# Loading the first block of a row sum in two DMAs, of 16 and of 112 partitions

One core of one Trainium2 chip runs the kernel. The metric is device time in microseconds (us), median over runs; lower is better.

## The reference

```python
x = np.random.randn(32, 512, 1024).astype(np.float32)   # 67.1 MB
multiplier = 0.5
def reference(x, multiplier):
    return (np.sum(x, axis=-1) * multiplier).astype(np.float32)
```

16,384 rows of 1024 numbers are summed. Every byte is read once and next to nothing is written (the page of before: 67.11 MB read, 0.07 MB written), so the time is about the time to read 67.1 MB.

## The kernel before

Each of the 128 partitions owns 112 consecutive rows, read in seven blocks of 16 rows (64 KB a partition, 8.4 MB a block), and 16 more rows that are read in smaller pieces at the end. (A partition is one of the 128 parts of SBUF, the memory on the chip; HBM is the memory that the input lies in. DMA engines copy from one to the other.) Three buffers rotate. VectorE reduces a block in one instruction; ScalarE helps at the end. The first three loads are moved ahead of the start-up code so that they are issued at once.

```python
    x_pool = ctx.enter_context(tc.tile_pool(name="x", bufs=3))
    ...
    for b in range(n_blocks - 1):
        c0 = b * B                                    # B = 16
        t = x_pool.tile([P, B, D], fp32, name="xb")
        loads.append(nc.sync.dma_start(out=t, in_=x_rows[:, c0 : c0 + B, :]))
        h = B if b < n_blocks - 2 else B // 2
        nc.vector.reduce_sum(
            out=sums[:, c0 : c0 + h], in_=t[:, 0:h, :], axis=mybir.AxisListType.X
        )
        nc.vector.tensor_single_scalar(...)           # times the multiplier
        ...                                           # ScalarE takes rows of the last full block
    ...                                               # the last 16 rows a partition: pieces of 8, 5, 2 rows,
                                                      # then the last row in two parts; two stores
    nc.at_finalize(start_loads_at_entry)              # loads that wait for nothing go first
```

## Time and profile before

| | before |
|---|---|
| time, median of 6 runs | 162.07 us (161.98 to 162.21) |
| span of the profiled run | 160.2 us |
| share of the 16 DMA engines that is busy | 97.6% |
| VectorE busy | 119.3 us (74%) |
| start of the first reduction | 21.83 us |
| packets of 64 KB (one partition of one block) after the first of each engine | 2.418 us (median; the longest 2.55) |

The last row is from the trace's record of DMA packets: a packet here is one partition's 64 KB of a block. The records give each packet's start and duration, not its engine or partition. The lines of the page, the timeline and the stretches are shown and read in the prediction. Two more lines are wanted for comparison: of the page the rate in 40 equal slices of the span, and of the timeline the last reduction:

```profile
GB/s 262 524 524 262 524 524 262 524 524 262 524 524 262 524 491 295 524 458 327 524 409 376 524 344 442 524 262 524 524 262 524 524 262 524 393 393 425 409 410 81
137.93 8.69 DVE L100 TENSOR_REDUCE sums<-xb 128x8 f32<-128x8192 f32 x1 [1.92 <-DMA xb<-in_x_dram]
```

A slice is 4 us and packets count in the slice where they start, so 16 packets come as 262, 32 as 524. The pattern 262, 524, 524 is a steady rate of some 437 on average, near the 16 x 27.1 = 434 of the prediction, and the rate keeps about that level from the first slice to the last but one.

### The profile page before, as it was taken

What the parts mean: (1) busy time and instruction counts of PE and PEld (TensorE: products, weight loads), DVE (VectorE), ACT (ScalarE), POOL (GpSimd) and SP (SyncE); (2) the same over time, 40 slices, a digit from 0 to 9 for tenths busy, and PEclk for the clock granted to TensorE, in tenths of its full rate; (3) what the DMA queues carried; (4) which work ended last, traced back from release to release, by engine and by line L of the source; (5) the groups of instructions that cost most, each with busy time, mean ns of one, the idle gap of its engine ahead of it and who ended that gap; (6) DMA issues with size and microseconds to landing.
All of it is one profiled execution on the core that took longest, in us unless ns stands there. A gap on an engine that the chain in (4) does not pass through costs nothing.

```text
span 160.2 us, 139 instructions
## 1 busy us (share of the span) xinstructions
DVE 119.3 (74%) x35; ACT 17.3 (11%) x31; POOL 0.2 (0%) x4
## 2 busy tenths in 40 slices
DVE  0000059997799968999599995999959999597443
ACT  0000000000000000000000000000000000599952
POOL 0000000000000000000000000000000000000000
DMA  7996996996996996997998979969969969999992
GB/s 262 524 524 262 524 524 262 524 524 262 524 524 262 524 491 295 524 458 327 524 409 376 524 344 442 524 262 524 524 262 524 524 262 524 393 393 425 409 410 81
DMA packets 2016, 67.18 MB, mean 419 GB/s; under 512 B 480, under 2 KB 608, under 8 KB 736
## 3 DMA queue, kind: packets, MB, share of 16 engines
q1 hardware_dynamic: 2016, 67.18, 97.6%
HBM read 67.11 MB, written 0.07 MB: 419 GB/s over the span
## 4 chain that ended last, share of the span: by engine, by line
DMA 75%; DVE 22%; SPq 1%; issue 0%; DVEq 0%
DMA xb<-in_x_dram 51%; DMA end<-in_x_dram 24%; DVE sums L100 22%; SPq L117 1%; DVE end L84 1%; SPq L98 0%; DVE res L103 0%; DVEq L63 0%; DVEq L208 0%
## 5 line engine op out<-in xcount | busy, mean ns | idle before, releaser
L100 DVE TENSOR_REDUCE sums<-xb 128x16 f32<-128x16384 f32 (+1 forms) x7 | 112.0, 16001 | 31.5 <-DMA xb<-in_x_dram 31.5
L74 ACT ACT_TABLE_LOAD x1 | 1.3, 1283 | 138.0 <-DMA xb<-in_x_dram 138.0
L74 ACT ACTIVATE xb<-xb 128x1024 f32<-128x1024 f32 x15 | 15.7, 1044 | 2.1 <-DMA xb<-in_x_dram 2.1
L84 DVE CUSTOM_DVE_ANT_0 xb<-xb 128x512 f32<-128x512 f32 x8 | 5.1, 688 | 5.0 <-DMA xb<-in_x_dram 5.0
L74 ACT ACTIVATION_READ_ACCUMULATOR xb<-xb 128x1 f32 x15 | 2.8, 186 | 0.0
L55 DVE MEMSET end<- 128x2 f32 x1 | 0.1, 60 | 1.8 <-PEq L194 1.8
L103 DVE TENSOR_SCALAR res<-sums 128x16 f32<-128x16 f32 (+1 forms) x7 | 1.2, 174 | 0.2
L84 DVE CUSTOM_DVE_ANT_0 end<-end 128x288 f32<-128x288 f32 (+1 forms) x2 | 0.9, 426 | 0.2
L84 DVE DVE_READ_ACCUMULATOR2_ANT res<- 128x1 f32 x9 | 0.7, 82 | 0.0
L194 POOL MEMSET const-bfloat16-1.0<- 128x1 bf16 x1 | 0.1, 102 | 0.0
L194 POOL MEMSET const-uint8-127<- 128x1 uint8 x1 | 0.1, 101 | 0.0
L194 POOL MEMSET const-float32-0.0<- 128x1 f32 x1 | 0.1, 99 | 0.2 <-issue 0.2
L194 POOL MEMSET const-float32-1.0<- 128x1 f32 x1 | 0.1, 98 | 0.0
L84 DVE DVE_READ_ACCUMULATOR2_ANT end<- 128x1 f32 x1 | 0.1, 82 | 0.0
## 6 DMA issues: line engine op xcount, KB each, us to landing
xb<-in_x_dram SPq DMA_DIRECT2D x1, 4096.0 KB, 31.1
xb<-in_x_dram SPq DMA_DIRECT2D x1, 2560.0 KB, 36.8
xb<-in_x_dram SPq DMA_DIRECT2D x1, 1024.0 KB, 38.9
end<-in_x_dram SPq DMA_DIRECT2D x1, 288.0 KB, 39.1
end<-in_x_dram SPq DMA_DIRECT2D x1, 224.0 KB, 39.1
xb<-in_x_dram SPq DMA_DIRECT2D x7, 40.8
out_dram<-res SPq DMA_DIRECT2D x1, 56.0 KB, 10.0
out_dram<-res SPq DMA_DIRECT2D x1, 8.0 KB, 1.4
```

Source lines behind the costliest of these rows:

```text
L55: nc.vector.memset(end[:, at - 2 : at], 0.0)
L74: acts.append(nc.scalar.activation(out=t[:, r, :], in_=t[:, r, :], func=mybir.ActivationFunctionType.Copy, scale=mul, accum_out=res[:, col ...
L84: return nc.vector.tensor_tensor_reduce(out=row[:, 0:mid], in0=row[:, 0:mid], in1=row[:, mid:], scale=scale, scalar=0.0, op0=ADD, op1=ADD, ...
L100: nc.vector.reduce_sum(out=sums[:, c0 : c0 + h], in_=t[:, 0:h, :], axis=mybir.AxisListType.X)
L103: nc.vector.tensor_single_scalar(out=res[:, c0 : c0 + h], in_=sums[:, c0 : c0 + h], scalar=mul, op=mybir.AluOpType.mult,)
L117: nc.sync.dma_start(out=t[:, lo:hi, :], in_=x_last[:, lo:hi, :])
L194: nc = _bacc.Bacc("TRN2", target_bir_lowering=False, num_devices=1)
```

## The change

The first block is to be loaded by two DMAs: one of 16 partitions, a single row of 64 KB for each DMA engine, and one of the other 112. The idea behind it is that a DMA with few rows is ready sooner, so that the sixteen engines start earlier and more evenly; since the engines are the bound (busy for 97.6% of the span), every idle moment at the start should be paid in full.

```diff
-        loads.append(nc.sync.dma_start(out=t, in_=x_rows[:, c0 : c0 + B, :]))
+        for lo, hi in ((0, 16), (16, P)) if b == 0 else ((0, P),):
+            loads.append(
+                nc.sync.dma_start(
+                    out=t[lo:hi], in_=x_rows[lo:hi, c0 : c0 + B, :]
+                )
+            )
```

## The prediction

> **What bounds the kernel now.** I read the page first: its shares of busy time, the table of DMA queues and the chain that ended last. Columns are explained by the lines themselves; "L" is a source line.
>
> ```profile
> span 160.2 us, 139 instructions
> DVE 119.3 (74%) x35; ACT 17.3 (11%) x31; POOL 0.2 (0%) x4
> q1 hardware_dynamic: 2016, 67.18, 97.6%
> DMA 75%; DVE 22%; SPq 1%; issue 0%; DVEq 0%
> ```
>
> The reader is to see that the DMA engines, at 97.6% of sixteen engines' time, bind, and that VectorE has room. The chain lists VectorE at 22%, but that is only how a chain through a three-buffer ring is followed back: a load is issued when a reduction frees its buffer, and then stands in a queue that is still full. The timeline of VectorE shows the true rhythm (start, duration, then in brackets the idle time before and its releaser):
>
> ```profile
> 21.83 17.22 DVE L100 TENSOR_REDUCE sums<-xb 128x16 f32<-128x16384 f32 x1 [19.96 <-DMA xb<-in_x_dram]
> 41.16 17.22 DVE L100 TENSOR_REDUCE sums<-xb 128x16 f32<-128x16384 f32 x1 [1.90 <-DMA xb<-in_x_dram]
> 60.52 17.22 DVE L100 TENSOR_REDUCE sums<-xb 128x16 f32<-128x16384 f32 x1 [1.94 <-DMA xb<-in_x_dram]
> ```
>
> Every reduction waits about 1.9 us for the DMA. The blocks land 41.16 - 21.83 = 19.33 us apart. A block is 128 partitions of 64 KB, so each of 16 engines moves 8 partition rows: one row takes **T = 19.33 / 8 = 2.416 us**, or 65,536 B / 2.416 us = 27.1 GB/s per engine. The first block lands at 21.83, and 21.83 - 19.33 = 2.5 us is its whole lead-in. I then cut the span into stretches (columns: length, busy time and instructions of DVE, ACT and POOL, clock, DMA share, GB/s; packets count where they start, which is why a stretch can exceed 1):
>
> ```profile
> 0.00:1.00 1.00, 0.00 (x0) 0.00 (x0) 0.20 (x4) 1.00 0.00 0
> 1.00:2.00 1.00, 0.06 (x1) 0.00 (x0) 0.00 (x0) 1.00 3.12 1049
> 21.80:41.20 19.40, 17.44 (x3) 0.00 (x0) 0.00 (x0) 1.00 1.00 432
> 118.50:137.90 19.40, 17.40 (x2) 0.00 (x0) 0.00 (x0) 1.00 0.94 405
> 137.90:157.00 19.10, 14.02 (x19) 16.92 (x30) 0.00 (x0) 1.00 0.98 414
> ```
>
> No data moves in the first microsecond. In the second, 1049 GB/s x 1 us = 1.05 MB start: exactly sixteen rows of 64 KB. All sixteen engines are already at work in that second microsecond, and from then on they never rest: 432 GB/s is 16 x 27.1. The packet records of the trace say it more finely: the sixteen first packets start within 0.51 us of each other, from 1.01 us after the first issue, and take 2.8 to 3.4 us (median 3.13), against 2.42 later. Last, the end of the chain:
>
> ```profile
> 117.89 39.08 DMA end<-in_x_dram
> 156.97 0.02 issue
> 156.99 0.48 DVE end L84 x2
> 157.61 0.39 DVE end L84
> ```
>
> The end hangs directly on the last load; only some 3.2 us follow it up to 160.2. An idle microsecond of the slowest engine anywhere in the run is a microsecond of the total.
>
> [...]
>
> **The change part by part.**
> It removes one DMA of 128 rows and adds one of 16 and one of 112. Bytes and row packets are the same (128 of 64 KB).
>
> Issue: one more DMA on SP, 0.33 us by the issue records, while the engines chew on the first: off the path, 0. VectorE waits for one more semaphore, 0.02 us by the records of such waits. The loads that follow keep their order, and blocks 1 and 2 are still issued at once.[...]
>
> Gain: [...]the stagger of 0.51 us and some of the 3.13 - 2.42 = 0.71 us of slow first packets could go: at most 1.2 us, I'd say 0.3.
>
> Cost, first DMA: [...]**3T = 7.25 us**.
>
> Cost, second DMA: [...]**2T = 4.83 us**. [...] That part rests on exact lockstep, so I take half, **2.4 us**.
>
> After that [...]the lag stays. Block 0 lands about 14 us late, and so does every buffer's release, but three buffers give 2 x 19.33 us of queued work, more than the reduction's 17.22 plus a lag difference of 10, so no engine starves. A reduction still fits in a block's period. Sum: 7.25 + 4.83 + 2.4 - 0.3 = 14.2 us, **162.1 + 14.2 = 176.3 us**.
>
> **The rivals.**
> A, nothing but the lead-in moves. [...]block 0 lands as before: 161.8 to 162.4. [...]
> B, the first DMA alone pays: [...] 162.1 + 7.25 = 169.4, or up to 172 with leftovers.
> C, the 112 are dealt out one by one (row i to engine i mod 16). [...]block 0 takes 8 x 4T = 77 us, 58 us more: 220. [...]
> D, the full lockstep: 3T + 4T = 16.9 us, 179.0.
>
> **The range and the chances.** I give A 0.25, B 0.25, my sum up to D 0.42, C or something else longer 0.08. A holds the result within 2% (3.2 us); B, D and C are all slower by over 2%. Faster by over 2% would need more than the whole 2.5 us of lead-in. Hence 176.3 us, range 161.6 to 181, faster 0.01, same 0.27, slower 0.72.
>
> **What would show it.** Right: the first reduction starts near 36 us, not 21.8; a stretch from 2 to 10 us shows about a quarter of 434 GB/s; the first sixteen packets take some 9.7 us; later gaps between reductions are back near 19.3; VectorE's total wait for the DMA rises by the lag, nearly all of it ahead of the first reduction[...]. If the first packets are long but the reduction starts near 29, B holds; at 77, C. It is wrong if the first reduction still starts near 21.8[...].

The marked passages are cut: which destination partitions slow each other down, and how the rows of a DMA are dealt to the engines; no trace shows it. The sum came to 7.25 + 4.83 + 2.4 - 0.3 = 14.2 us, and 162.1 + 14.2 = 176.3. Its first three terms (3T for the first DMA, 2T for the second, half of another 2T on the way into block 1) stand as what was forecast, not as what any run shows; the 0.3 is a guess.

## The result

| | before | after |
|---|---|---|
| time, median of 6 runs | 162.07 us | 184.08 us (183.53 to 184.36) |
| ratio | | 1.1353 (95% interval 1.1334 to 1.1373) |

A ratio here is the mean time of one kernel's fast runs over that of the other's of the same rounds, so it isn't quite the ratio of the medians. The kernel is 13.5% slower, 22.0 us. Lines of the page of after:

```profile
span 182.3 us, 141 instructions
GB/s 230 14 216 230 244 417 201 230 216 288 446 460 460 460 417 360 403 446 460 446 460 460 431 403 360 446 446 460 446 460 460 417 403 360 439 446 392 431 361 16
q1 hardware_dynamic: 2032, 67.18, 97.1%
```

The same 67.18 MB are moved, and the engines are busy for the same share of a longer span: 97.1%. The busy share therefore says nothing of the loss; the rate does. For the first ten slices (4.56 us each, 46 us) it is about half of what it is later. The timeline of VectorE of after, with the first three reductions and the last, says when the loss occurs:

```profile
44.09 17.22 DVE L106 TENSOR_REDUCE sums<-xb 128x16 f32<-128x16384 f32 x1 [41.55 <-DMA xb<-in_x_dram]
63.35 17.22 DVE L106 TENSOR_REDUCE sums<-xb 128x16 f32<-128x16384 f32 x1 [1.83 <-DMA xb<-in_x_dram]
82.71 17.22 DVE L106 TENSOR_REDUCE sums<-xb 128x16 f32<-128x16384 f32 x1 [1.93 <-DMA xb<-in_x_dram]
...
160.10 8.69 DVE L106 TENSOR_REDUCE sums<-xb 128x8 f32<-128x8192 f32 x1 [1.92 <-DMA xb<-in_x_dram]
```

The first reduction starts 44.09 - 21.83 = 22.3 us later than before. After it the spacing is 19.26 and 19.36 us, as before, and the last one is 160.10 - 137.93 = 22.2 us late. All of the loss falls into the load of the first block; nothing is made up or added later. Stretches of after (the last column is GB/s of packets that start there):

```profile
1.00:2.00 1.00, 0.00 (x0) 0.00 (x0) 0.00 (x0) 1.00 8.57 1049
2.00:8.00 6.00, 0.06 (x1) 0.00 (x0) 0.00 (x0) 1.00 0.00 0
8.00:12.00 4.00, 0.00 (x0) 0.00 (x0) 0.00 (x0) 1.00 1.33 262
```

In the second microsecond sixteen rows start (1.05 MB), as before. Then no engine starts another row for six microseconds; the next sixteen begin between 8 and 12 us. The packet records give the rows of the first block in the order in which each engine took them ("took" is the median of the 16 engines, in us; "last end" is when the slowest engine was done with the row). The records don't name the engine; the rows are strung together by their times, as each starts within 0.03 us of the end of another:

| row of an engine | before: took | after: took | before: last end | after: last end |
|---|---|---|---|---|
| 1 | 3.13 | 8.44 | 4.54 | 10.95 |
| 2 | 2.42 | 5.35 | | |
| 3 | 2.42 | 4.73 | | |
| 4 | 2.42 | 3.19 | | |
| 5 | 2.42 | 3.87 | | |
| 6 | 2.42 | 4.50 | | |
| 7 | 2.42 | 4.79 | | |
| 8 | 2.42 | 4.54 | 21.45 | 43.40 |
| 9 (block 1) | 2.42 | 3.35 | 23.87 | 45.85 |

On the slowest engine the first row lost 10.95 - 4.54 = 6.4 us, the seven rows of the second DMA (43.40 - 10.95) - (21.45 - 4.54) = 15.5 us, and the first row of block 1 nothing more: together 22.0 us. What the change was made for didn't come either: the sixteen first packets start 1.015 to 1.824 us after the first issue, against 1.014 to 1.520 before.

### The profile page after: what moved, and what is told of

The parts are those of the page before. It is cut to its first block, busy times and chain, and to the rows that moved or that the text cites. A ratio compares the mean times of both kernels' runs of the same rounds, so it can differ in the third digit from the quotient of the medians.

```text
span 182.3 us, 141 instructions
## 1 busy us (share of the span) xinstructions
DVE 119.3 (65%) x35; ACT 17.3 (9%) x31; POOL 0.2 (0%) x4
## 2 busy tenths in 40 slices
DMA packets 2032, 67.18 MB, mean 369 GB/s; under 512 B 496, under 2 KB 624, under 8 KB 752
## 3 DMA queue, kind: packets, MB, share of 16 engines
q1 hardware_dynamic: 2032, 67.18, 97.1%
## 4 chain that ended last, share of the span: by engine, by line
DMA 68%; DVE 29%; another core or an unknown queue 1%; SPq 1%; issue 0%; DVEq 0%
DMA xb<-in_x_dram 68%; DVE sums L106 28%; DVE end L85 0%; DVE xb L85 0%; SPq L123 0%; SPq L101 0%; DVE res L109 0%; DVEq L64 0%; DVEq L106 0%; DVE res L85 0%; DVEq L214 0%
```

## The experiments

Two rows are said to collide here if they are under way at the same time and slow each other down because of the partitions that they are written to. Which ones do so was assumed; the list is cut from the expectations below, and their figures for SHARE and JAM that come from it stand as what was expected only. The theory behind the forecast, SHARE, was that rows that collide share one engine's rate and the others go on undisturbed. It comes near the first row (7.25 us forecast, 6.4 measured), but gives the second DMA a third of what it cost (4.83 of 15.5). Its rivals were JAM (one collision holds up all sixteen engines), MEMORY (the spacing of the source rows in HBM is what matters, not the destination) and DEAL (the 112 rows go to the engines otherwise than seven consecutive ones each).

The probes replace the whole body of the kernel by loads into one tile and return zeros. After each step VectorE reads a column of the tile, and the next step's load waits for that mark. So the time from mark to mark is that of one step with its issue and landing. In the lines below the width of a mark's output counts the steps, and the idle time in brackets is the time of the step.

### Sixteen rows at a time (e1_probe16)

```diff
+    load(out=t, in_=far)                      # step 1: 128 partitions
+    load(out=t[0:16], in_=far[0:16])          # 2: 16 neighbours
+    load(out=t[0:16], in_=near[0:16])         # 3: the same, source rows adjoin
+    load(out=t[32:96:4], in_=far[0:16])       # 4: every 4th from 32
+    load(out=t[0:128:8], in_=far[0:16])       # 5: every 8th
+    load(out=t[0:112:7], in_=far[0:16])       # 6: every 7th
+    load(out=t[0:80:5], in_=far[0:16])        # 7: every 5th
+    load(out=t[0:32], in_=far[0:32])          # 8: 32 neighbours
```

> A probe of loads alone, each waiting for a mark on VectorE that the one before has landed; the result is zeros on purpose. T = 2.42 us is one 64 KB row on an engine, and each step has some 2.5 us of issue and landing. Four theories. SHARE: [...] JAM: [...] MEMORY: [...]it is the spacing of the source rows in HBM. DEAL: the rows go to the engines otherwise than seven consecutive ones each. Step 2 (16 neighbouring partitions[...]): all but MEMORY 4T + 2.5 = 12.2 us. Step 3 (the same from adjoining source rows): 12.2, but MEMORY 4.9. Step 4 (the source of step 2 to partitions 32, 36 ... 92[...]): SHARE, JAM, DEAL 4.9 to 5.6, MEMORY 12.2. Step 5 (every 8th partition[...]): 2T + 2.5 = 7.3, MEMORY 12.2. Step 6 (every 7th[...]): lands after 7.3; SHARE has twelve packets of 2.4 to 3.1 us and four of 4.8, JAM sixteen near 4.8. Step 7 (every 5th[...]): the same with six short under SHARE, none under JAM. Step 8 (32 neighbours, two rows an engine): 12.2 if consecutive rows go to one engine, 8T + 2.5 = 21.8 if they are dealt out one by one.

Measured, timeline of VectorE:

```profile
22.56 0.15 DVE L43 TENSOR_SCALAR mark<-xb 128x1 f32<-128x1 f32 x1 [21.57 <-DMA xb<-in_x_dram]
...
34.42 0.17 DVE L43 TENSOR_SCALAR mark<-xb 128x2 f32<-128x2 f32 x1 [11.71 <-DMA xb<-in_x_dram]
46.28 0.17 DVE L43 TENSOR_SCALAR mark<-xb 128x3 f32<-128x3 f32 x1 [11.68 <-DMA xb<-in_x_dram]
52.35 0.17 DVE L43 TENSOR_SCALAR mark<-xb 128x4 f32<-128x4 f32 x1 [5.91 <-DMA xb<-in_x_dram]
60.60 0.17 DVE L43 TENSOR_SCALAR mark<-xb 128x5 f32<-128x5 f32 x1 [8.09 <-DMA xb<-in_x_dram]
68.02 0.17 DVE L43 TENSOR_SCALAR mark<-xb 128x6 f32<-128x6 f32 x1 [7.24 <-DMA xb<-in_x_dram]
75.93 0.17 DVE L43 TENSOR_SCALAR mark<-xb 128x7 f32<-128x7 f32 x1 [7.74 <-DMA xb<-in_x_dram]
88.98 0.17 DVE L43 TENSOR_SCALAR mark<-xb 128x8 f32<-128x8 f32 x1 [12.88 <-DMA xb<-in_x_dram]
```

Steps 2 and 4 load the same sixteen source rows. To sixteen neighbouring partitions they take 11.71 us, to partitions 32, 36, ... 92 they take 5.91. Step 3 changes the source instead and changes nothing (11.68). MEMORY falls: the destination partitions set the time of the first DMA. Step 8 takes 12.88, not the 21.8 expected of rows dealt out one by one. (Two rounds of step 2 come to the like: 2 x (11.71 - 2.5) + 2.5 = 20.9 us, an estimate from step 2 and the lead-in of 2.5.) Step 6 decides between SHARE and JAM: by the packet records no row took less than 3.5 us (3.5 to 5.2, median 3.98), where SHARE wanted twelve of 2.4 to 3.1; in step 4 they took 2.7 to 3.7. Step 7: 4.2 to 5.3. That goes against SHARE, though step 6 isn't the sixteen rows near 4.8 that JAM wanted either.

### The 112 rows by themselves (e2_probe112)

```diff
+    load(out=t, in_=far)                      # step 1: 128 partitions
+    load(out=t[16:128], in_=far[16:128])      # 2: the second DMA of the change
+    load(out=t[16:128], in_=near[16:128])     # 3: the same, source rows adjoin
+    load(out=t[0:112], in_=far[16:128])       # 4: to the first 112 partitions
+    for j in range(7):                        # 5: every 7th partition, seven DMAs
+        nc.sync.dma_start(out=t[16 + j : 128 : 7], in_=far[16 + j : 128 : 7])
+    seen()
+    load(out=t[0:64], in_=far[0:64])          # 6: half of the partitions
+    load(out=t, in_=near)                     # 7: 128 partitions
```

> A probe of loads alone, as before; zeros on purpose. Steps 1 and 7 (128 partitions, spaced and adjoining rows): 8T + 2.5 = 21.8 us. Step 2 (partitions 16 to 127, the second DMA of the change): SHARE 9T + 2.5 = 24.2; JAM 14T + 2.5 = 36.3[...]; dealt one by one 28T, 70. Step 3 (the same from adjoining rows): as step 2, but MEMORY 19.4. Step 4 (the same rows to partitions 0 to 111): as step 2. Step 5 (seven DMAs of 16 rows, every 7th partition[...]): as step 2 if the DMA of 112 gives each engine seven consecutive rows; different under DEAL. Step 6 (64 partitions[...]): 8T + 2.5 = 21.8 for half the bytes of step 7.

Measured, timeline of VectorE:

```profile
57.80 0.17 DVE L43 TENSOR_SCALAR mark<-xb 128x2 f32<-128x2 f32 x1 [35.03 <-DMA xb<-in_x_dram]
...
91.41 0.17 DVE L43 TENSOR_SCALAR mark<-xb 128x3 f32<-128x3 f32 x1 [33.44 <-DMA xb<-in_x_dram]
124.61 0.17 DVE L43 TENSOR_SCALAR mark<-xb 128x4 f32<-128x4 f32 x1 [33.03 <-DMA xb<-in_x_dram]
...
159.93 0.17 DVE L43 TENSOR_SCALAR mark<-xb 128x5 f32<-128x5 f32 x1 [35.15 <-DMA xb<-in_x_dram]
...
183.24 0.17 DVE L43 TENSOR_SCALAR mark<-xb 128x6 f32<-128x6 f32 x1 [23.14 <-DMA xb<-in_x_dram]
205.31 0.17 DVE L43 TENSOR_SCALAR mark<-xb 128x7 f32<-128x7 f32 x1 [21.90 <-DMA xb<-in_x_dram]
```

112 partitions alone (35.03) take 13 us longer than 128 (21.90). The source matters little (33.44). Seven DMAs of every seventh partition, which were to impose the supposed order, take 35.15, like the one of 112: nothing is left that speaks for DEAL, though the records name no engine and so don't show the deal itself. SHARE wanted 24.2, JAM 36.3. Half of the partitions (0 to 63, 23.14) take longer than all of them, with 5.12 us a row.

### The same split along the rows of the batch (e3_cols)

```diff
-        for lo, hi in ((0, 16), (16, P)) if b == 0 else ((0, P),):
+        for lo, hi in ((0, 2), (2, B)) if b == 0 else ((0, B),):
-                    out=t[lo:hi], in_=x_rows[lo:hi, c0 : c0 + B, :]
+                    out=t[:, lo:hi, :], in_=x_rows[:, c0 + lo : c0 + hi, :]
```

> The first block is cut by rows of the batch instead of by partitions: two of sixteen for all 128 partitions, then the other fourteen. [...] SHARE, JAM and DEAL: the time of before, 162.1 us, within 0.6. A theory that two DMAs for the first block cost by themselves (the extra issue, a second semaphore[...]): some of the 22 us.

Measured: 161.92 us against 162.07, ratio 0.9987 (0.9975 to 1.0). Two DMAs and one more issue cost nothing; it is the cut between partitions that does.

### The first block in halves (e4_halves)

```diff
-        for lo, hi in ((0, 16), (16, P)) if b == 0 else ((0, P),):
+        for lo, hi in ((0, 64), (64, P)) if b == 0 else ((0, P),):
```

> The first block is cut into partitions 0 to 63 and 64 to 127. SHARE and JAM agree if consecutive rows go to an engine: [...]16T instead of 8T: 162.1 + 19.3 = 181.4 us. If rows are dealt out one by one[...], 32T: 220. MEMORY and a cost of the split itself: no reason for so much, the time of before or of the change's few rows.

Measured: 183.56 us, ratio 1.1324 (1.1306 to 1.1341): 21.5 us more, against 19.3 expected. The row of 5.12 us from the probe accounts for it: 8 rows x (5.12 - 2.42) = 21.6. SHARE and JAM expected the same here, so it doesn't tell one from the other.

### How many engines are slowed (e5_probe_few)

```diff
+    load(out=t, in_=far)                                  # step 1
+    for j in range(32, 36):                               # step 2; then from 28, 24, 16 and 0
+        nc.sync.dma_start(out=t[j : j + 61 : 4], in_=far[j : j + 61 : 4])
+    seen()
...
+    load(out=t[32:96], in_=far[32:96])                    # step 7
```

> A probe of loads alone; zeros on purpose. Each step but the first and last is four DMAs of 16 partitions, every 4th one, with one row for each engine in each. Step 2 starts at partition 32: [...]4T + 3.4 = 13.1 us (3.4 is what the single clean row of the first probe took beyond T). Step 3 starts at 28[...]. Step 4 starts at 24[...]. Step 5 at 16[...]. Step 6 at 0: [...]4 x 5.12 + 2.7 = 23.1 us. SHARE: steps 3 to 5 land like step 6, but the packets of the lone engines stay at 2.4 us: 14, 12 and 8 of the 16 in each DMA. JAM: hardly any packet of steps 3 to 5 stays at 2.4, and their mean is near the 4.7 of the DMA of 112. Step 7 (partitions 32 to 95 in one DMA[...]): 13.1 us, against 23.1 for partitions 0 to 63.

Measured, timeline of VectorE (steps 2, 3, 4, 6 and 7):

```profile
35.03 0.17 DVE L43 TENSOR_SCALAR mark<-xb 128x2 f32<-128x2 f32 x1 [12.36 <-DMA xb<-in_x_dram]
...
56.47 0.17 DVE L43 TENSOR_SCALAR mark<-xb 128x3 f32<-128x3 f32 x1 [21.27 <-DMA xb<-in_x_dram]
...
79.48 0.17 DVE L43 TENSOR_SCALAR mark<-xb 128x4 f32<-128x4 f32 x1 [22.84 <-DMA xb<-in_x_dram]
...
125.45 0.17 DVE L43 TENSOR_SCALAR mark<-xb 128x6 f32<-128x6 f32 x1 [22.82 <-DMA xb<-in_x_dram]
...
137.94 0.17 DVE L43 TENSOR_SCALAR mark<-xb 128x7 f32<-128x7 f32 x1 [12.32 <-DMA xb<-in_x_dram]
```

By the marks alone, step 3 (from 28, 21.27) looks nearly as bad as step 6 (from 0, 22.82), as both theories have it, because the step ends with its slowest engine. The packet records tell what the other engines did: in step 3 the median row of each DMA after the first took 2.418 us and only the rows of two engines took 4.8; in step 4 (from 24) not one of 64 rows took less than 4.4, the median 5.09, like step 6. So step 3 is as SHARE has it and step 4 as JAM has it, and neither holds for both. That was not among the theories. Step 7 shows that 64 partitions in one DMA run at the full 2.42 us a row if they are 32 to 95 (12.32 us, against 23.14 for 0 to 63 in the probe before).

### A cut with partitions 32 to 95 by themselves (e6_mid)

```diff
-        for lo, hi in ((0, 16), (16, P)) if b == 0 else ((0, P),):
+        for lo, hi in ((32, 96), (0, 32), (96, P)) if b == 0 else ((0, P),):
```

> The first block in three DMAs: partitions 32 to 95 ([...]4 rows at 2.42 us), then 0 to 31 and 96 to 127 ([...]5.12 us a row by the second probe). SHARE and JAM: 162.1 + 4 x (5.12 - 2.42) = 172.9 us, half of what the halves cost, though there are more DMAs. If every DMA of fewer than 128 partitions were slow: 8 x 2.7 = 21.6 more, 183.7.

Measured: 172.79 us, ratio 1.0662 (1.0645 to 1.0678). Three DMAs cost half of what two cost in the halves (10.75 us more than before, where 4 x (5.12 - 2.42) = 10.8 was expected).

### Two blocks cut (e7_two)

```diff
-        for lo, hi in ((0, 16), (16, P)) if b == 0 else ((0, P),):
+        for lo, hi in ((0, 16), (16, P)) if b < 2 else ((0, P),):
```

> The suspected cost doubled: blocks 0 and 1 are both cut into 16 and 112 partitions. If each cut block costs its own time[...], 162.1 + 2 x 22.0 = 206 us. A cost of the start alone, which the first block bears once: 184.

Measured: 206.52 us, ratio 1.2741 (1.2724 to 1.2758); 206.52 - 162.04 = 44.5, or 2 x 22.2. The timeline of VectorE has the second reduction 39.3 us after the first, where it used to be 19.3:

```profile
46.55 17.22 DVE L106 TENSOR_REDUCE sums<-xb 128x16 f32<-128x16384 f32 x1 [43.22 <-DMA xb<-in_x_dram]
...
85.82 17.22 DVE L106 TENSOR_REDUCE sums<-xb 128x16 f32<-128x16384 f32 x1 [21.84 <-DMA xb<-in_x_dram]
```

The second cut block costs about as much as the first, so the cost isn't one of the start. The two can't be told apart to the microsecond: 24.7 us of it come before the first reduction (22.3 in after) and 19.9 between the two.

### What the change wanted, without its cost (e8_cols1)

```diff
-        for lo, hi in ((0, 2), (2, B)) if b == 0 else ((0, B),):
+        for lo, hi in ((0, 1), (1, B)) if b == 0 else ((0, B),):
```

(The diff is against e3_cols.)

> What the change wanted[...]: one row of the batch (4 KB) for all 128 partitions first, then the other fifteen. By the run with two rows first, whose first reduction started 0.07 us earlier than before, 162.0 us, within 0.5 of before.

Measured: 161.83 us against 162.04, ratio 0.9992 (0.9979 to 1.0004): no difference to speak of. The first reduction starts at 21.72 us instead of 21.83, and the first packets still come 1.00 us after the first issue. This smoother start gained some 0.1 us at the first reduction, and nothing that can be told from noise in the time. Whether some other start would gain more, no run tells.

### One pair or two, at other places (e9_probe_pairs)

```diff
+    for k in range(3):                        # t is three tiles wide here
+        nc.sync.dma_start(out=t[32:93:4, k], in_=far[0:128:8])   # step 2
+    seen()
...                                            # from, step of 3 to 10:
...                                            # 28,4  36,4  4,7  18,7 | 24,4  40,4  24,5  22,7
```

> A probe of loads alone; zeros on purpose. Each step but the first is three DMAs of the same 16 partitions (into three thirds of the tile) from the same source rows[...]. Step 2: nobody shares. Steps 3 to 6: one pair shares[...]. Steps 7 to 10: two pairs share[...]. The probe before gave SHARE with one pair and JAM with two, at one place each. NUMBER (two pairs jam all engines, one pair none): in steps 3 to 6 the fourteen lone engines keep 2.42 us a row after the first and the marks come after 6T + 3 = 17 to 18 us or a little more; in steps 7 to 10 all sixteen engines take 4.7 to 5.2 us a row and the marks come after 18 us. PLACE[...]: some of 3 to 6 jam, or some of 7 to 10 don't.

(A pair that shares is two engines whose rows were expected to collide. Which rows do was assumed in laying out the steps.)

Measured, timeline of VectorE for steps 2, 3 and 7 (expected: no pair, one, two; three columns a step, so widths of 6, 9 and 21):

```profile
71.69 0.17 DVE L43 TENSOR_SCALAR mark<-xb 128x6 f32<-128x6 f32 x1 [10.10 <-DMA xb<-in_x_dram]
89.35 0.17 DVE L43 TENSOR_SCALAR mark<-xb 128x9 f32<-128x9 f32 x1 [17.49 <-DMA xb<-in_x_dram]
...
158.06 0.17 DVE L43 TENSOR_SCALAR mark<-xb 128x21 f32<-128x21 f32 x1 [17.58 <-DMA xb<-in_x_dram]
```

and the first 8.5 us of data of the same three steps (length, busy times of DVE and POOL, clock, DMA share, GB/s):

```profile
62.90:71.40 8.50, 0.00 (x0) 0.00 (x0) 1.00 0.93 370
73.10:81.60 8.50, 0.00 (x0) 0.00 (x0) 1.00 0.95 355
141.70:150.20 8.50, 0.00 (x0) 0.00 (x0) 1.00 1.10 247
```

370 GB/s x 8.5 us is 48 rows: all have started. In step 3 it is 46, so only two third rows are missing. In step 7 it is 32: all sixteen engines are a row behind. The packet records have the same for all eight places (us, median of the second and third rows of an engine, and the slowest row):

| step | pairs expected | median row | rows under 2.6 us, of 48 | slowest row |
|---|---|---|---|---|
| 2 | none | 2.418 | 33 | 3.36 |
| 3, 4, 5, 6 | one | 2.418 in each | 28, 29, 28, 29 | 4.83 to 5.13 |
| 7, 8, 9, 10 | two | 4.93 to 5.21 | 0, 0, 0, 0 | 4.97 to 5.34 |

(In step 2 an engine's first row takes about 3.1 us, which is why 33 and not 48 are under 2.6.) What NUMBER expected came at all eight places, and what PLACE expected at none: in steps 3 to 6 the other fourteen engines kept to 2.418 us, in steps 7 to 10 all sixteen were held up. For four of the places that can be put without the assumption. One partition of step 2's sixteen exchanged (28 for 92, or 96 for 32) slowed two engines; two exchanged (24 and 28 for 88 and 92, or 96 and 100 for 32 and 36) slowed all sixteen. In steps 7 to 10 the first rows are held up less, with medians of 4.2 to 4.5 us; that fits step 6 of the first probe, which had first rows alone (3.98). By which mechanism it happens is not shown, and no run here tells it.

## Why the prediction was wrong

- **What bounds the kernel, and that nothing is made up later.** Right: 22.3 us at the first reduction, 22.2 at the last, 22.0 in time.
- **Gain of at most 1.2 us, guessed 0.3.** In the change nothing came of it, since the first packets start no earlier. Where the start is smoothed with all 128 partitions in each DMA it is 0.1 us at the first reduction (21.72 against 21.83).
- **First DMA, 3T = 7.25 us.** Nearly right in size: 6.4 us on the slowest engine. By step 4 against steps 2 and 3 of the first probe (5.91 us against 11.71 and 11.68) the cause is where the rows are written, not where they are read. Why these partitions are slow together is not shown.
- **Second DMA, 2T = 4.83 us.** This is the step that failed. The forecast let only rows that collide pay for it, while the others go on at T: the term measured 15.5 us in place of 4.83. The last probe has destinations of both kinds, some that slow two engines and leave fourteen at 2.418 us a row, and some that slow all sixteen, to medians of 4.93 to 5.21. The 112 alone have slow and shorter rows in turn: medians of 4.70, 4.74, **3.04, 3.87**, 4.57, 4.72, 4.51 us, 30.15 together, 13.2 more than 7T. Sent to partitions 0 to 111, the short rows move one place on: 4.79, 4.73, 4.76, **3.22, 3.31**, 4.57, 4.71. The slowest engine of after paid more than the medians: its row 4 took 4.78 us, where fourteen engines took 2.93 to 3.34, its row 5 took 3.74 and the other five rows 24.0. The author's count of which rows meet in which step rested on the assumed list and is left out: why two rows are the short ones is not shown. That most engines took 2.9 to 3.9 us in rows 4 and 5, when the last probe has 2.42, may be because the engines are no longer in step; that is argued, not shown.
- **Crossing into block 1, 2.4 us.** Wrong: 0.0 on the slowest engine. The other engines took 2.8 to 3.7 us for the first row of block 1 (median of all 3.35), but the slowest one, which came to it last, took 2.45.
- **The rivals.** A (only the lead-in moves) had the first block land as before, near 21.8 us, and C (dealt one by one) needed 77 us for it; it landed at 44. B and D were counted with SHARE and fall with it. No rival had engines slowed whose own rows were not expected to collide, so the top of the range, 181, was too low.

## What to carry to other kernels

Cut a load that is bound by the DMA engines along the free dimension, with all 128 partitions in each part, rather than between partitions: the first block in two DMAs cost 22 us one way and nothing the other (184.08 and 161.92 us against 162.07). If fewer partitions have to be loaded, time the sets in question: here partitions 32 to 95 in one DMA ran at 2.42 us a row and 0 to 63 at 5.12, and exchanging one or two of sixteen partitions made the difference between no engine slowed, two, and all sixteen. And the busy share of the DMA engines doesn't show it, as it was 97.1% with the cut and 97.6% without: read GB/s in stretches and the durations of packets.
